# Two more buffers for the up weights, the last row tiles' sums ordered later, two norm factors later

## Chip, cores and metric

The kernel runs on one core of a Trainium2 chip. The metric is the device time of one execution in microseconds. Before the change it took 2193.57 us (median of 3 runs, 2191.82 to 2195.93).

## The reference

One inference step of a two-layer decoder of width 1024, for a prompt of 1024 tokens and 8 single decode tokens (1032 columns in all). Layer 0 mixes tokens by gated linear attention beside cross-attention into 256 memory tokens; layer 1 by sliding-window attention, again beside memory attention, with keys and values projected from the residual stream after layer 0. After each mixer stands a squared-ReLU MLP of width 4096 between two norms, and the change touches this MLP alone:

```python
def squared_relu_mlp(h, w_up, w_down):
    return jnp.square(jax.nn.relu(h @ w_up)) @ w_down
...
    f = squared_relu_mlp(rmsnorm(x, norm_ffn_pre[l]), w_ffn_up[l], w_ffn_down[l])
    x = x + rmsnorm(f, norm_ffn_post[l])
```

## The kernel before

Activations lie feature-major: 128 partitions by 8 feature tiles by token columns. Every float32 operand is split into a high part (a cast, `split` L157, on ScalarE) and a low part (source minus high part, on VectorE), and every product is three matmuls: high by high, high by low, low by high.

`mlp` (L678) is called once per layer. Its up product first makes 4 of the 32 row tiles of the hidden width directly (`up_plain`, L708) and stores the squared ReLUs in `apd`. The other 28 row tiles are taken in 14 pairs by a Strassen-Winograd scheme of seven products on half the features and half the columns (516, in two pieces of 258). `XF` holds the seven combinations of activations, made by `steps` (L766). `items` (L828) runs over pairs and products. For each pair `prepare` (L831) loads two raw weight tiles `ws` of 512 KB (`wstage`, L227, a pool of two buffers) and lets `wino_weights` (L657) make the seven weight combinations one after another, in place in the raw tiles, each split into a slot of three weight buffers. So the raw tiles are free only after the pair's last split. `prepare` runs up to five products ahead. `product` (L840) issues the 24 matmuls (L820 to L822) of one product into six rotating PSUM banks and the evictions (L641 to L655) on VectorE and ScalarE. After a pair, `factors` (L856) makes three more combinations of the pair's four result rows on VectorE, and `store` (L863) writes all seven into `awd` in DRAM. During pairs 2 to 4 `square_mean` (L727) also computes statistics of the residual.

The four direct row tiles need their combinations too. `plain_factors` (L871) is a generator: for each of two groups it loads four tiles `c` from `apd` (L875), makes four sums (L882) and stores each into `awd` (L883). It is advanced once per phase of the down product, in the first 13 phases.

The down product runs 64 phases (`phase`, L1034): six products of 8 phases over the hidden width with all 516 columns (48 matmuls per phase, L1050 to L1052), and one product in two column halves (`s` = 0 and 1, 8 phases of 24 matmuls each). Each phase needs a row tile `ra` read back from `awd` (`load_a`, L965, two buffers, asked for three phases ahead) and a weight tile `wr` (`load_w`, L978, five ahead; the first two lie in the same two-buffer pool as `ws`). `prep` (L986) splits both, two phases ahead. `gather` (L1016) adds the finished products into four accumulators.

The end of the MLP is the post-norm, done in four pieces pa to pd (`Closing`, L327), each of which squares its piece, sums over partitions by a matmul with ones (`Stats.mean`, L195, matmul L205), finishes the inverse root (`finish`, L210) and then scales and adds the residual (`close`). `hook` (L1085) starts these in given phases of the last product.

The order of the work is set by a list scheduler at compile time. It takes instructions by priority (program order, moved forward in `high_priority` blocks) on a model of the engines; each engine and each DMA queue then executes its list in order. Two means bend this order. A manual dependency marked NOSYNC adds no semaphore: it only keeps an instruction behind another one in the scheduler's order. `tick` (L127) uses it: `Stats.mean` is given a number of matmul columns, and its matmul is put behind the matmul in which that number has been counted down. One unit is 3 x 8 x 384 = 9216 columns. All the loads and stores named here are issued by SyncE's queue (SP).

Of the kernel before, what the change touches and what calls it, by code (L numbers as in the profile page):

```python
# [8 lines left out]
F32 = mybir.dt.float32  # L9
# [7 lines left out]
P = 128  # L17
# [19 lines left out]
PAIRS = [(m, m + 1) for m in range(NPL, DFF // P, 2)]  # L37
# [12 lines left out]
def hybrid_decoder_step(ctx: ExitStack, tc: tile.TileContext, A, O):  # L50
    nc = tc.nc
# [13 lines left out]
    rp = ctx.enter_context(tc.tile_pool(name="rstd", bufs=1))  # L65
# [26 lines left out]
    def nm(s):  # L92
        uid[0] += 1
        return f"{s}_{uid[0]}"
# [132 lines left out]
    def wstage(src, pool=None):  # L227
        with tc.high_priority(WPRI):
            ws = (pool or wp).tile([P, KT, P], F32, tag="ws", name=nm("ws"))
            nc.sync.dma_start(ws, src)  # L230
            return ws
# [446 lines left out]
    def mlp(l, X, ff):  # L678
# [4 lines left out]
        left, right = ff.left, ff.right  # L683

        def pool(st, side, name, bufs=1):
            return st.enter_context(tc.tile_pool(name=nm(name), bufs=bufs, side=side, reuse_waits="tile"))
# [21 lines left out]
        def up_plain(c):  # L708
            hl = X[c][0]
            c0, n = CH[c]  # L710
            for m in range(NPL):
                ps = mmps()
                proj(ps, W[m], hl, n, low_last=(m == NPL - 1))
                with first():
                    t = tmp3([P, 2, n])
                    nc.scalar.activation(t[:, 0, :], ps[:, :n], AF.Relu)
                    nc.scalar.activation(t[:, 1, :], t[:, 0, :], AF.Square)
                    if c < 2:
                        nc.sync.dma_start(apd[l, :, m, c, :384], t[:, 1, :])
                    else:  # L720
                        nc.sync.dma_start(apd[l, :, m, :, 384:], t[:, 1, :].rearrange("p (h w) -> p h w", h=2))
# [23 lines left out]
        def home(pool, tag, n=4):  # L745
            return pool.tile([P, n, HALF], F32R, tag=tag, name=nm("xf"))

        def cut(i, b, p):
            hi, lo = XF[i]
            eng = nc.vector  # L750
            p = pieces[p]
            for j in range(2):
                ks = slice(2 * j, 2 * j + 2)
                src = p[b][:, ks, :]
                if not isinstance(lo, list):
                    split(hi[:, ks, p["at"]], lo[:, ks, p["at"]], src, eng)
                    continue
                nc.scalar.copy(hi[:, ks, p["at"]], src)
                for k in (2 * j, 2 * j + 1):
                    eng.tensor_tensor(lo[k][:, p["at"]], p[b][:, k, :], f32(hi[:, k, p["at"]]), ALU.subtract)  # L760
# [5 lines left out]
        def steps(p):  # L766
            cut(1, "b11", p)
            comb(p, "b12", "b22", "b12", ALU.subtract)
            yield
            cut(7, "b12", p)  # L770
            comb(p, "b11", "b12", "b11", ALU.add)
            yield
            if p == 0:
                s0 = home(xp, "xh0", 5)
                XF[6] = (home(fa, "t2h"), s0[:, :4])
                XF["s0"] = s0
            cut(6, "b11", p)
            comb(p, "b12", "b22", "b11", ALU.subtract)
            yield
            if p == 0:  # L780
                s0 = XF.pop("s0")
                s1, s2 = home(xp, "xl0", 5), home(xp, "xh1", 5)
                s3 = home(xp, "xl1", 5)
                XF[5] = (s1[:, :4], s2[:, :4])
                XF[2] = (s3[:, :4], [x[:, 4] for x in (s0, s1, s2, s3)])
            cut(5, "b12", p)
            yield
            cut(2, "b21", p)
            comb(p, "b21", "b11", "b21", ALU.subtract)
            yield  # L790
            if p == 0:
                XF[3] = (home(xp, "xh2"), home(xp, "xl2"))
            cut(3, "b22", p)
            yield
            if p == 0:
                ff.rest.close()
                t4 = pool(right, "right", "t4")
                XF[4] = (home(t4, "h"), home(t4, "l"))
            cut(4, "b21", p)
            yield  # L800

        up_plain(0)
        scale(0)
        scale(1)
# [21 lines left out]
            return t[:, SUB * s : SUB * s + SUB]  # L826

        items = [(j, i) for j in range(len(PAIRS)) for i in ORDER]  # L828
        ws, gens, made = {}, {}, [0]

        def prepare(upto):  # L831
            while made[0] < min(upto, len(items)):
                j, i = items[made[0]]
                made[0] += 1
                if j not in gens:
                    w1, w2 = (wstage(A["w_up"][l, m]) for m in PAIRS[j])
                    gens[j] = wino_weights(w1[:, :4], w1[:, 4:], w2[:, :4], w2[:, 4:], slots)
                ws[j, i] = next(gens[j])

# [31 lines left out]
        def plain_factors():  # L871
            for q in range(2):
                rows = [tp.tile([P, 768], F32, tag=tag, name=nm("c"))[:, :HALF] for tag in ("t3", "t3", "tq", "tq")]
                for r, (m, h) in zip(rows, ((0, 0), (0, 1), (1, 0), (1, 1))):
                    nc.sync.dma_start(r, apd[l, :, 2 * q + m, h, :])  # L875
                yield
                yield
                c11, c12, c21, c22 = rows
                for f_, r, a, b, op in ((1, c12, c22, c12, ALU.subtract), (4, c11, c12, c11, ALU.add),
                                        (6, c21, c11, c21, ALU.subtract), (5, c22, c22, c11, ALU.subtract)):  # L880
                    yield
                    TT(r, a, b, op)  # L882
                    nc.sync.dma_start(awd[l, f_, NJ - 1, :, q, :], r)  # L883
# [201 lines left out]
        def hook(v):  # L1085
            if -8 <= v < -4:
                split(*lasting(v + 8), reg(3, v + 8))
            if v == -4:
                pa.feed(0, 1, 2, 3)
            if v == 0:  # L1090
                rooms((pa, "xh0"), (pc, "xl0"))
                pa.factor(rp.tile([P, 384], F32, tag="rf", name=nm("rf")), 0.3 * unit)
            if v == 1:
                pb.feed(0, 1, 2, 3)
                pb.factor(rx, 2 * unit)
            if v == 2:
                pa.close(behind=kept["mm"])
            if v == 4 and not l:
                hl[0] = xtiles(0)
                pa.cut(hl)  # L1100
            if v == 5:
                rooms((pb, "xl2"))
                pb.close(behind=kept["mm"])
            if v == 7:
                pc.feed(2, 3, 0, 1)
                pc.factor(rb, 2.5 * unit)
            if v == 9:
                pc.close((2, 3, 0, 1), behind=kept["mm"])
            if v == 11:
                rooms((pd, "xh2"))  # L1110
            if v == 10 and not l:
                rt[0] = rtile(0)
                pa.measure(0, rt[0], 2.3 * unit, Ring())
            if v == 11 and not l:
                hl[1] = xtiles(1)
                pc.cut(hl)
                hl[2] = xtiles(2)
                pb.cut(hl)
# [10 lines left out]
        for t in range(N):  # L1129
            for u in ([3, 4, 5] if t == 0 else [t + 5]):  # L1130
                if u < N:
                    load_w(u)
            if t + 3 < N:
                load_a(t + 3)
            if t + 2 < N:
                with urgent(2) if t + 2 >= 6 * NJ else ExitStack():
                    prep(t + 2)
            if t < 13:
                next(plain, None)
            phase(t)  # L1140
            if l == 0 and t in folds:
                fold(folds.pop(t), kept["mm"])
            hook(t - 6 * NJ)

        st2.close()
        if l:
            with urgent(2):
                pd.finale()
                pd.factor(rp.tile([P, 384], F32, tag="rf", name=nm("rf"))[:, : pd.n], 0)
            pd.close()  # L1150
        else:
            xs = pool(st, "right", "xs", 3)
            mq = pool(st, "right", "mq", 2)
            pd.feed(2, 3, 0, 1)
            pd.factor(rp.tile([P, 384], F32, tag="rf", name=nm("rf"))[:, : pd.n], 2 * unit)
            pd.close((2, 3, 0, 1), xs)
            pd.cut(hl, (2, 3, 0, 1))
            rt[1] = rtile(1)
            pc.measure(1, rt[1], 4 * unit, mq)
            pd.measure(1, rt[1], 5 * unit, mq)  # L1160
            rt[2] = rtile(2)
            pb.measure(2, rt[2], 9 * unit, mq)
            pd.measure(2, rt[2], 10 * unit, mq)
            res = [(hl[c], rt[c]) for c in range(3)]
# [1052 lines left out]
```

## Time and profile before

| | |
|---|---|
| median of 3 runs | 2193.57 us |
| profiled execution, own time | 2196.19 us |
| its span | 2194.4 us |
| TensorE busy | 97% |
| VectorE busy | 68% |
| ScalarE busy | 49% |
| mean granted TensorE clock | 0.994 |
| up products of the pairs, layer 0 / 1 | 536.9 to 826.3 us / 1566.2 to 1851.5 us |
| down products, layer 0 / 1 | 828.0 to 1157.1 us / 1852.2 to 2179.8 us |

The times of the two last rows are the first and last starts of the matmuls of lines L820 to L822 and L1050 to L1052. In the profile "PE" is TensorE, "DVE" VectorE, "ACT" ScalarE, "SPq" the queue of SyncE, "PEclk" the granted clock as a share of the full one. In timelines a bracket gives the idle time of the engine ahead of the instruction and what ended it. In a view by windows each engine has its busy time and, in brackets, its instructions; then come PEclk, the mean share of the 16 DMA engines and GB/s.

### The profile page before, as it was taken

The page shows a single profiled execution, that of the slowest core. Times are in us where ns is not written, and L with a number is a line of the kernel's source. Part 1 is how long each engine was busy: PE and PEld are TensorE (multiplying, and loading weights), DVE is VectorE, ACT ScalarE, POOL GpSimd, SP SyncE. Part 2 cuts the span into 40 slices and gives each one's busy share as a digit, 9 for nine tenths or more (in the row PEclk, how much of TensorE's full clock was granted, in tenths as well). Part 3 has the DMA queues.
Part 4 walks back from the last instruction along what each step waited for, and adds up shares of the span by engine and source line. Part 5 has one row for each costly group of instructions (what it writes and reads, how often), then busy time and mean ns, then how long its engine had stood idle before and what let it go on. Part 6 is the DMA issues. An engine that isn't in the chain of part 4 may idle for free.

```text
span 2194.4 us, 41861 instructions
## 1 busy us (share of the span) xinstructions
PE 2137.5 (97%) x16918; PEld 2040.5 (93%) x16918; DVE 1502.1 (68%) x2839; ACT 1083.3 (49%) x2191; POOL 112.4 (5%) x170
## 2 busy tenths in 40 slices
PE   8999999999999999999999999899999999999997
PEld 6879999999999999999999878699999999999997
DVE  7546648668877677756787455747888777855767
ACT  6354536457645444334554354646655445333453
POOL 0012000000000000034000000200000000000001
PEclk9999999999999999999999999999999999999999
DMA  4422026542664449467355101424275446725344
GB/s 168 143 68 75 24 65 176 157 140 98 189 216 130 153 157 328 143 225 237 117 156 164 53 21 32 164 71 149 97 241 183 141 160 219 268 97 167 100 132 145
DMA packets 142823, 316.40 MB, mean 144 GB/s; under 512 B 15833, under 2 KB 58897, under 8 KB 142273
## 3 DMA queue, kind: packets, MB, share of 16 engines
q1 hardware_dynamic: 125216, 270.43, 38.6%
q0 software_dynamic: 8368, 30.42, 4.2%
q10 hardware_dynamic: 9040, 12.82, 1.6%
q8 instruction: 134, 2.20, 0.4%
q14 instruction: 65, 0.53, 0.1%
HBM read 220.97 MB, written 93.74 MB: 143 GB/s over the span
## 4 chain that ended last, share of the span: by engine, by line
PE 70%; DVE 11%; DMA 11%; ACT 5%; issue 3%; SPq 0%; DVEq 0%; ACTq 0%
PE mm L259 16%; PE mx L259 8%; DMA ws<-in_w_up 5%; PE mx L1050 5%; PE mx L1051 5%; PE mx L1052 5%; DVE wl L159 3%; PE mm L1050 2%; PE mm L1051 2%; PE mm L1052 2%; PE mx L820 2%; PE mx L821 2%; PE mx L822 2%; DMA ra<-awd 1%; ACT wh L158 1%
## 5 line engine op out<-in xcount | busy, mean ns | idle before, releaser
L158 ACT CAST wh<-ws 128x512 fp32r<-128x512 f32 (+1 forms) x258 | 184.1, 721 | 304.8 <-DVE ws L666 119.7
L820 PE MATMUL mx<-xf,wh 128*128 128x258 f32 x1048 | 297.9, 284 | 3.7 <-DVE aw L649 3.5
L821 PE MATMUL mx<-xf,wh 128*128 128x258 f32 x1048 | 295.6, 282 | 0.0
L822 PE MATMUL mx<-xf,wl 128*128 128x258 f32 x1048 | 295.5, 282 | 0.0
L259 PE MATMUL mm<-xh,wh 128*128 128x384 f32 (+1 forms) x864 | 282.0, 326 | 1.6 <-DVE acc L1032 1.1
L259 PE MATMUL mm<-xh,wl 128*128 128x384 f32 (+1 forms) x864 | 278.5, 322 | 0.0
L259 PE MATMUL mm<-xl,wh 128*128 128x384 f32 (+1 forms) x864 | 278.1, 322 | 0.0
L159 DVE TENSOR_TENSOR wl<-ws,wh 128x512 fp32r<-128x512 f32 (+1 forms) x258 | 208.6, 816 | 100.6 <-ACT wh L158 100.3
L158 ACT CAST wh<-wr 128x1024 fp32r<-128x1024 f32 x102 | 106.9, 1048 | 283.7 <-PE sx L1051 271.1
L1050 PE MATMUL mx<-sa,wh 128*128 128x258 f32 x840 | 239.2, 285 | 5.2 <-ACT sa L158 1.8
L159 DVE TENSOR_TENSOR wl<-wr,wh 128x1024 fp32r<-128x1024 f32 x102 | 125.4, 1229 | 171.0 <-ACT wh L158 170.6
L1051 PE MATMUL mx<-sa,wh 128*128 128x258 f32 x840 | 236.9, 282 | 1.8 <-DVE sa L159 1.8
L1052 PE MATMUL mx<-sa,wl 128*128 128x258 f32 x840 | 236.7, 282 | 0.0
L820 PEld LDWEIGHTS mx<-xf,wh 128*128 128x128 f32 x1048 | 197.6, 189 | 5.6 <-DVE aw L649 5.1
L821 PEld LDWEIGHTS mx<-xf,wh 128*128 128x128 f32 x1048 | 198.0, 189 | 0.4
L822 PEld LDWEIGHTS mx<-xf,wl 128*128 128x128 f32 x1048 | 197.9, 189 | 0.0
L259 PEld LDWEIGHTS mm<-xh,wh 128*128 128x128 f32 x864 | 162.8, 188 | 10.9 <-issue 7.5
L259 PEld LDWEIGHTS mm<-xh,wl 128*128 128x128 f32 x864 | 162.4, 188 | 7.5 <-issue 5.5
L259 PEld LDWEIGHTS mm<-xl,wh 128*128 128x128 f32 x864 | 162.8, 188 | 6.8 <-issue 6.0
L1050 PEld LDWEIGHTS mx<-sa,wh 128*128 128x128 f32 x840 | 159.4, 190 | 7.1 <-DVE aw L655 2.5
L159 DVE TENSOR_TENSOR sa<-ra,sa 128x1032 fp32r<-128x1032 f32 (+1 forms) x128 | 144.2, 1126 | 27.1 <-ACT sa L158 26.6
L1051 PEld LDWEIGHTS mx<-sa,wh 128*128 128x128 f32 x840 | 159.2, 190 | 2.3 <-DVE sa L159 2.2
(569 smaller groups left out, 5792.7 us busy)
## 6 DMA issues: line engine op xcount, KB each, us to landing
ra<-awd SPq DMA_DIRECT2D x92, 516.0 KB, 3.7
ws<-in_w_up SPq DMA_DIRECT2D x64, 512.0 KB, 4.4
wr<-in_w_downb SPq DMA_DIRECT2D x64, 512.0 KB, 6.0
awd<-aw SPq DMA_DIRECT2D x26, 1032.0 KB, 7.7
awd<-am SPq DMA_DIRECT2D x28, 774.0 KB, 9.2
ws<-in_w_in_a SPq DMA_DIRECT2D x20, 512.0 KB, 3.9
ws<-in_w_out SPq DMA_DIRECT2D x16, 512.0 KB, 3.6
t<-xd SPq DMA_DIRECT2D x20, 384.0 KB, 3.6
```

What stands on the lines that cost most here:

```text
L158: nc.scalar.copy(hi, src)
L159: (eng or nc.vector).tensor_tensor(lo, src, f32(hi), ALU.subtract)
L259: mm = nc.tensor.matmul(ps[:M, :n], w_[:, k, :M], x_[:, k, :], start=(i == 0), stop=(i == 3 * KT - 1))
L820: nc.tensor.matmul(ps, wh(k), xh, start=(k == 0), stop=False)
L821: nc.tensor.matmul(ps, wh(k), xl, start=False, stop=False)
L822: mm = nc.tensor.matmul(ps, wl(k), xh, start=False, stop=(k == n - 1))
L1050: nc.tensor.matmul(ps, wh[:, q, ms], h, start=(jj == 0 and q == 0), stop=False)
L1051: nc.tensor.matmul(ps, wh[:, q, ms], lo, start=False, stop=False)
L1052: mm = nc.tensor.matmul(ps, wl[:, q, ms], h, start=False, stop=end)
```

## The change

The up weights of pairs 1, 3, 5 and so on go into a second pool of two buffers, `wq`, which is opened where the last combination of activations gets its room. `fetch` loads a pair's two tiles, and once that pool is open, the preparation of pair j also asks for the tiles of pair j+1. Next, the loads in `plain_factors` are put, by NOSYNC dependencies, behind the last matmul issued so far, and the generator is advanced after the phase's matmuls where it was advanced before them. Last, the matmul of piece pc's norm factor is put behind 2.8 units of later columns where it was 2.5, and that of piece pd in layer 0 behind 2.7 where it was 2.

```diff
                 t4 = pool(right, "right", "t4")
                 XF[4] = (home(t4, "h"), home(t4, "l"))
+                stage[0] = pool(right, "right", "wq", 2)
             cut(4, "b21", p)
             yield
 
+        stage = [None]
         up_plain(0)
...
-        ws, gens, made = {}, {}, [0]
+        ws, gens, made, raw = {}, {}, [0], {}
+
+        def fetch(j):
+            if j not in raw and j < len(PAIRS):
+                raw[j] = [wstage(A["w_up"][l, m], stage[0] if j % 2 else None) for m in PAIRS[j]]
 
         def prepare(upto):
...
                 if j not in gens:
-                    w1, w2 = (wstage(A["w_up"][l, m]) for m in PAIRS[j])
+                    fetch(j)
+                    w1, w2 = raw[j]
+                    if stage[0]:
+                        fetch(j + 1)
                     gens[j] = wino_weights(w1[:, :4], w1[:, 4:], w2[:, :4], w2[:, 4:], slots)
...
                 for r, (m, h) in zip(rows, ((0, 0), (0, 1), (1, 0), (1, 1))):
-                    nc.sync.dma_start(r, apd[l, :, 2 * q + m, h, :])
+                    d = nc.sync.dma_start(r, apd[l, :, 2 * q + m, h, :])
+                    tc.add_manual_dep(d.ins, kept["mm"], NOSYNC, reason="behind later matmuls")
...
                 pc.feed(2, 3, 0, 1)
-                pc.factor(rb, 2.5 * unit)
+                pc.factor(rb, 2.8 * unit)
...
+            phase(t)
             if t < 13:
                 next(plain, None)
-            phase(t)
...
-            pd.factor(rp.tile([P, 384], F32, tag="rf", name=nm("rf"))[:, : pd.n], 2 * unit)
+            pd.factor(rp.tile([P, 384], F32, tag="rf", name=nm("rf"))[:, : pd.n], 2.7 * unit)
```

## The prediction

> **What bounds the kernel now.** The first two lines of the page come first: the span and the engines' busy shares.
>
> ```profile
> span 2194.4 us, 41861 instructions
> PE 2137.5 (97%) x16918; PEld 2040.5 (93%) x16918; DVE 1502.1 (68%) x2839; ACT 1083.3 (49%) x2191; POOL 112.4 (5%) x170
> ```
>
> TensorE (PE) is the bound, and the change removes no matmul, so only time that PE loses can be won. Busy time hides half of that loss, because a matmul that starts late is drawn longer. So I count matmuls by stage. The second view is busy time by windows, PE alone; "x" is the count. The windows are the middle and end of the up products and the first 13 us of the down products, of layer 0 and then of layer 1.
>
> ```profile
> 560.00:600.00 40.00, 40.00 (x336) 1.00 0.74 225
> 600.00:665.00 65.00, 62.32 (x503) 1.00 0.63 203
> 665.00:826.40 161.40, 160.19 (x1332) 1.00 0.47 152
> 826.40:840.00 13.60, 10.02 (x55) 0.75 0.89 347
> 1580.00:1645.00 65.00, 65.00 (x542) 1.00 0.67 216
> 1645.00:1851.60 206.60, 205.60 (x1705) 1.00 0.50 163
> 1851.60:1865.00 13.40, 9.61 (x60) 0.87 0.96 362
> ```
>
> The first row is a stretch without loss: 336 matmuls in 40 us, 8.4 per us, 0.119 us each. At that pace the other rows lack 43, 24, 59, 4, 30 and 53 matmuls, which is 5.1, 2.8, 7.0, 0.5, 3.6 and 6.3 us. Part of the up rows is no loss: three pairs of statistics matmuls per layer, one of them here from the chain of waits, take 0.65 us a pair where their count of two stands for 0.24.
>
> ```profile
> 622.58 0.65 PE sx L205 x2
> ```
>
> That takes off 3 x 0.4 = 1.2 us per layer. What is left is 6.7 us of loss in layer 0's up stage and 2.9 in layer 1's (9.6 together), and 7.0 + 6.3 = 13.3 us at the two changes from up to down. That is all this change can reach, apart from the norm factors below.
>
> Why PE loses in the up stage: the timelines of VectorE (DVE) and PE.
>
> ```profile
> 614.70 0.69 DVE L666 TENSOR_TENSOR ws<-ws,ws 128x512 f32<-128x512 f32 x1 [2.25 <-DMA ws<-in_w_up]
> 615.65 0.42 DVE L649 TENSOR_TENSOR aw<-mx,aw 128x258 f32<-128x258 f32 x1
> 616.12 0.39 PE L820 MATMUL mx<-xf,wh 128*128 128x258 f32 x1 [0.79 <-DVE aw L649]
> 637.58 0.69 DVE L666 TENSOR_TENSOR ws<-ws,ws 128x512 f32<-128x512 f32 x1 [3.62 <-DMA ws<-in_w_up]
> 639.00 0.39 PE L820 MATMUL mx<-xf,wh 128*128 128x258 f32 x1 [1.42 <-DVE aw L649]
> ```
>
> DVE works in order. The first combination of a pair's weights (L666) waits 2.25 and 3.62 us for the second up tile; the evictions (L649) stand behind it, PSUM banks stay full, PE waits 0.79 and 1.42 us. The chain of waits shows why this returns with each pair:
>
> ```profile
> 691.80 7.29 DMA ws<-in_w_up
> 712.06 7.30 DMA ws<-in_w_up
> ```
>
> One buffer's loop (load 7.3 us, then 13 us until the last split frees it) takes 20.3 us, while PE needs 14 x 12 = 168 matmuls x 0.119 = 20.0 us for a pair. The load decides by 0.3 us, and any disturbance is never made good.
>
> **The change part by part.**
>
> **Two more weight buffers.** Nothing is added on a computing engine: the same 28 weight loads of 512 KB per layer, half of them into new buffers, and each pair's issued when the pair before starts its preparation, which is when its own load would have been issued for that earlier pair. The 7.3 us load then has 20 us of cover, and L666 no longer waits; the loop left is PE's own. Bounds: from the page, the plain idle time ahead of the largest group of these matmuls, 3.5 us, and the whole count, 9.6.
>
> ```profile
> L820 PE MATMUL mx<-xf,wh 128*128 128x258 f32 x1048 | 297.9, 284 | 3.7 <-DVE aw L649 3.5
> ```
>
> Layer 0's worst stretch has L666 waits in front of it, so I stand nearer the count, but keep something for evictions behind splits: **-7 us**. With its cover gone, that is if the new buffers came free only when they are needed, the load would cost what it costs now, 9.6 us. At the start two pairs are fetched together (4 x 512 KB); if DVE waited once for this, the price is one wait as above, 2.25 to 3.62 us behind which PE loses 0.8 to 1.4.
>
> **What follows at the change from up to down.** The last pair (13) is odd, so it lies in the new buffers; the old two, where the first two down weights (wr) also go, come free a pair earlier. SyncE's queue (SP), ScalarE (ACT) and PE at that place, and the windows of DMA and of the clock:
>
> ```profile
> 812.99 0.33 SPq L982 DMA_DIRECT2D wr<-in_w_downb  x1
> 813.42 0.39 SPq L865 DMA_DIRECT2D awd<-aw  x1
> 814.81 0.33 SPq L982 DMA_DIRECT2D wr<-in_w_downb  x1
> 815.19 1.46 SPq L869 DMA_DIRECT2D awd<-am  x1
> 816.75 1.59 SPq L976 DMA_DIRECT2D ra<-awd  x2
> 826.87 1.05 ACT L158 CAST sa<-ra 128x1032 fp32r<-128x1032 f32 x1 [4.69 <-DMA ra<-awd]
> 827.97 0.39 PE L1050 MATMUL mx<-sa,wh 128*128 128x258 f32 x1 [1.37 <-ACT sa L158]
> 829.24 0.38 PE L1051 MATMUL mx<-sa,wh 128*128 128x258 f32 x1 [0.88 <-DVE sa L159]
> 816.00:826.00 10.00, 10.00 (x86) 10.00 (x85) 4.01 (x10) 2.33 (x3) 0.00 (x0) 1.00 1.05 347
> 828.00:836.00 8.00, 5.79 (x21) 4.65 (x22) 8.00 (x11) 7.31 (x10) 0.00 (x0) 0.60 0.81 315
> ```
>
> The first down product waits for its row tile ra. Its 10 us are queueing: 2 x 512 KB of wr, 1032 KB and 774 KB of stores and 2 x 516 KB of ra, 3.86 MB, share full DMA engines (share 1.05) at 347 GB/s: 11.1 us. With both wr gone a pair earlier, where the share is 0.47, 2.84 MB are left, 8.2 us: ra lands 2.9 us sooner, at 824. Cast (1.05) and low part (1.22, the row of such a split stands below) end at 826.2, and PE finishes its up products at 826.6 (827.97 less its wait of 1.37). The waits of 1.37 and 0.88 go. The later ones, for evictions queued behind those splits on DVE, shrink, and with them the stretch at clock 0.60, whose cost is the other half of the 7.0 us. Bounds per layer: nothing (the engines stay saturated with the stores) to all 7.0 and 6.3. I leave 2.4 us per layer, one split of 1.2 us between evictions at half clock: **-8.5 us** for both.
>
> [...]
>
> **Last row tiles' sums later.** Per layer 8 loads, 8 subtractions or additions and 8 stores (258 KB each) leave the up stage and go behind the first (four) and the seventh (four) down phase.
>
> ```profile
> L882 DVE TENSOR_TENSOR c<-c,c x16: 683/689/697, 619.1 to 1677.5; 128x516 f32<-128x516 f32 x16
> SPq L883 <- DVE aw L651: 9.6, 1, 9.6
> SPq L883 <- DVE c L882: 5.7, 3, 3.0
> 862.42 1.05 ACT L158 CAST wh<-wr 128x1024 fp32r<-128x1024 f32 x1 [3.69 <-PE sx L1051]
> 865.62 1.22 DVE L159 TENSOR_TENSOR sa<-ra,sa 128x1032 fp32r<-128x1032 f32 x1
> 866.00:872.00 6.00, 5.90 (x6) 1.00 0.93 350
> ```
>
> On DVE that is 8 x 0.69 = 5.5 us per layer out of the stage where it holds PE up, which is inside the 7 us above. In the down stage a phase is 48 matmuls, 5.7 us; its splits are ready 4.4 us after the weight slot frees (862.42 to 866.84) and are needed two phases after (11.4 us), so 7 us of slack hide 5.5 us even in the stretch where DVE is full (5.90 of 6 us). The 4.1 MB are 11.8 us of DMA at 350 GB/s, spread over 13 phases (74 us); the first quarter comes while the engines are near full (0.81 at 828 to 836, 0.93 at 866 to 872), but the row loads run three phases ahead. Cost **0**; bounds 0 and, without that cover, 5.5 us per layer on DVE, or the SP price in the last rival.
>
> **Norm factors later.** 0.3 units (unit: 9216 columns) is 4 groups of three matmuls, 1.4 us; 0.7 units is 6452 columns or 17 matmuls of 384 columns at 0.173 us, 2.9 us.
>
> ```profile
> 1143.75 0.70 PE L205 MATMUL sf<-rb,ones 128*128 128x258 f32 x2 [0.69 <-DVE rb L199]
> 1158.40 0.41 PE L259 MATMUL mm<-xh,wh 128*128 128x384 f32 x1 [1.06 <-DVE acc L1032]
> 1175.11 0.70 PE L205 MATMUL sx<-rf,ones 128*128 128x258 f32 x2 [2.27 <-DVE rf L199]
> 1186.09 2.46 DVE L159 TENSOR_TENSOR xl<-acc,xh 128x264 fp32r<-128x264 f32 x7 [0.74 <-ACT xh L158]
> 1187.51 0.34 PE L259 MATMUL sT<-xh,wh 128*128 128x384 f32 x1
> ```
>
> Both waits are in layer 0 and end: 0.69 < 1.4 and 2.27 < 2.9. But what hangs on these factors is late next. The factor of 1175.11 would start 0.6 us later by the clock (2.9 - 2.27); the last splits of the next stage's input (1186 to 1188.5) follow it through a full DVE, and PE takes up that second chunk at 1187.51, just as its splits arrive. PE gets there 2.3 us sooner and waits for it. Likewise the factor of 1143.75 moves 0.7 us later, and the end of its chain, an eviction behind it on DVE, already holds PE 1.06 us at 1158.40. Bounds: -3 us (both waits gone, other matmuls fill in) to +1.3 us (both chains late). I take the middle of the mechanism, **0**. In layer 1 no such wait shows, and 1.4 us of delay stays ahead of the last evictions.
>
> **The sum.** -7 - 8.5 + 0 + 0 = -15.5 us. The profiled execution took 2196.19 us (1.8 around the span): 2180.7. It lies 2.6 us above the median of the runs, 2193.57, so against the median the forecast is 2178; I say **2179 us**.
>
> **The rivals.** First, **the queue at the change of stages stays** (for: the stores still fill the engines there, and the order on SP may keep wr where it is; against: a buffer freed 20 us earlier). Then only the up stage gains: 2193.6 - 7 = 2186.6. Second, **all lost time comes back**: 9.6 + 13.3 + 3 = 26 us, 2168; for it speaks that PE runs whole stretches of 40 us without loss, against it that evictions still share DVE with splits. Third, **the loads come no sooner in effect**, since SP is in order and a load for the new buffers stands behind stores that wait for DVE: the L666 waits return elsewhere, 2191 to 2194. Fourth, on the other side, **SP is blocked in the down stage**: each of the 8 stores per layer waits in SP's queue for its DVE operation, with row and weight loads behind it. Before, four such waits took 15.3 us, 3.8 each. Eight in a row are 30 us per layer; above the 7 us of slack plus one phase (5.7) PE loses what remains, 18 us per layer, 36 in all, less 15.5: 2214. It decides only if the waits follow each other without the queue recovering; over 13 phases with 9 us between stores that is unlikely.
>
> **How the numbers follow.** The forecast has 0.50 (its own range 2174 to 2184), the first rival 0.20, the second 0.12, the third 0.11, the fourth and lesser stalls 0.07. The range 2168 to 2191 holds the forecast and the first two rivals with the bounds of the unknown costs, and the better edge of the third. Faster by over 0.2% (4.4 us, about what a measurement of this kernel can tell from no change): 0.50 + 0.20 + 0.12 = 0.82; within 0.2%: 0.11; slower: 0.07.
>
> **What would show it.** Right: no DVE L666 wait on ws of more than a few tenths; 600 to 665 us with 540 matmuls; wr issued some 20 us before the last aw store; ra landing in 7 us or less; no clock below 0.9 at the change of stages; the two L205 waits gone and a wait at the second chunk's first matmul instead. Wrong: wr still between the two stores; PE waiting for sa in the first 13 down phases; SP held for several us at L883 there; or the up rows as short of matmuls as now.

## The result

The changed kernel takes **2173.97 us** (median of 4 runs, 2170.10 to 2175.46) against 2194.75 us before (4 runs beside it, 2191.82 to 2201.47). The ratio is 0.9898, 95% interval 0.9872 to 0.9925: 1.0% faster. Its profiled execution took 2174.24 us, of which 2172.3 us are the span. The forecast was 2179.0 us with a range of 2168 to 2191, so the time lies inside, 5 us on the fast side and at the lower edge of the narrower range, 2174 to 2184, that went with the forecast's own chance.

The first lines of the page of the changed kernel, as before: the span and the busy shares.

```profile
span 2172.3 us, 41879 instructions
PE 2126.8 (98%) x16918; PEld 2034.8 (94%) x16918; DVE 1520.1 (70%) x2839; ACT 1090.2 (50%) x2191; POOL 112.2 (5%) x170
```

PE has the same 16918 matmuls and is drawn as busy for 10.7 us less, while the span fell by 22.1: the busy time shows only half of it. Where that happened is seen in the windows of PE alone, in the same stretches of layer 0 and layer 1 as before, shifted by what was gained up to there (columns: length, PE's busy time and matmuls, granted clock, DMA share, GB/s).

```profile
600.00:665.00 65.00, 65.00 (x541) 1.00 0.51 158
817.90:831.50 13.60, 13.60 (x117) 1.00 1.00 349
1632.70:1836.30 203.60, 203.60 (x1697) 1.00 0.46 153
1836.30:1849.70 13.40, 13.40 (x115) 1.00 1.01 353
```

At 8.4 matmuls per us the first 13.6 us of the down product should hold 114 matmuls. They held 55 and now hold 117, at clock 1.00 instead of 0.75; layer 1 has 115 of 113 where it had 60. The stretch from 600 to 665 us holds 541 of 546 (503 before), and the missing five are no more than the statistics matmuls take. No loss is left in these rows; the one of layer 1's up stage lacks 13 of 1710 matmuls, 1.6 us, of which the two statistics pairs in it make 0.8; the rest is within the rounding of the pace (one matmul more or less in the 40 us from which it was taken is 5 in this row). The whole span, cut at the first and last matmuls of the stages:

| stretch | before, us | after, us | difference |
|---|---|---|---|
| start to first up product of layer 0 | 536.9 | 534.5 | -2.4 |
| up products, layer 0 | 289.4 | 283.3 | -6.1 |
| change and down products, to the next stage's first matmul | 332.1 | 326.0 | -6.1 |
| next stage to first up product of layer 1 | 407.8 | 409.1 | +1.3 |
| up products, layer 1 | 285.3 | 283.3 | -2.0 |
| change, down products and end | 342.9 | 336.1 | -6.8 |

The sum is -22.1 us. No edit lies in the first row, and in the fourth only the norm's last factor. What differs in both is the granted clock: it was 0.50 for 3.4 us from 99.1 us on in the profile before and never in this row in the one after; in the fourth row it was 0.50 for 6.8 us before (from 1392.8 on) and for 10.2 us after (from 1377.9 on). Half the clock for 3.4 us is 1.7 us by estimate, most of the -2.4 and as much as the +1.3. Two executions of one kernel, the one with the sums alone below, lie 4.1 and 4.4 us apart in these two rows. So the edits' own gain is in the other four rows, 21.0 us.

The timeline of the changed kernel, with the rows that answer those of the stalls before: VectorE's first combination of a pair's weights, then SP's queue at the end of layer 0's up products and ScalarE's cast of the first row tile.

```profile
623.51 0.69 DVE L666 TENSOR_TENSOR ws<-ws,ws 128x512 f32<-128x512 f32 x1
...
779.54 0.33 SPq L992 DMA_DIRECT2D wr<-in_w_downb  x1
782.00 0.33 SPq L992 DMA_DIRECT2D wr<-in_w_downb  x1
...
799.79 0.37 SPq L874 DMA_DIRECT2D awd<-aw  x1
801.33 2.52 SPq L986 DMA_DIRECT2D ra<-awd  x2
...
808.73 1.05 ACT L158 CAST sa<-ra 128x1032 fp32r<-128x1032 f32 x1 [1.18 <-DMA ra<-awd]
```

L666 has no bracket: the tile is there. The two wr leave 20 and 18 us before the last aw store (before, 0.4 us ahead of it and 1.4 us behind it). The row tile is asked for at 801.33 and its cast starts at 808.73, 7.4 us later (before 10.1). The up products end at 817.9, the first down matmul's start. The cast therefore starts 9.2 us before PE needs its first down product; before, it started 0.3 us too late (826.87 against 826.6).

The norm's place, PE's timeline, where the prediction quoted waits of 0.69, 1.06 and 2.27 us:

```profile
1128.98 0.70 PE L205 MATMUL sf<-rb,ones 128*128 128x258 f32 x2 [0.33 <-DVE rb L199]
1143.84 0.41 PE L259 MATMUL mm<-xh,wh 128*128 128x384 f32 x1 [2.70 <-DVE acc L1042]
1158.71 0.70 PE L205 MATMUL sx<-rf,ones 128*128 128x258 f32 x2 [1.77 <-DVE rf L199]
1172.50 0.35 PE L259 MATMUL sT<-xh,wh 128*128 128x384 f32 x1
1181.89 0.39 PE L259 MATMUL sA<-xh,wh 128*128 128x264 f32 x1 [0.65 <-DVE kf L1846]
```

The two factor waits are shorter, not gone, the eviction's wait has grown from 1.06 to 2.70, and the second chunk (1172.50) waits for nothing.

### The profile page after: what moved, and what is told of

Its sections match the earlier page's. It is cut to its first block, busy times and chain, and to the rows that moved or that the text cites. A ratio compares the mean times of both kernels' runs of the same rounds, so it can differ in the third digit from the quotient of the medians.

```text
span 2172.3 us, 41879 instructions
## 1 busy us (share of the span) xinstructions
PE 2126.8 (98%) x16918; PEld 2034.8 (94%) x16918; DVE 1520.1 (70%) x2839; ACT 1090.2 (50%) x2191; POOL 112.2 (5%) x170
## 4 chain that ended last, share of the span: by engine, by line
PE 88%; DVE 4%; ACT 3%; DMA 3%; issue 1%; SPq 0%; DVEq 0%; ACTq 0%
PE mm L259 16%; PE mx L259 8%; PE mx L822 6%; PE mx L824 6%; PE mx L823 6%; PE mx L1060 5%; PE mx L1061 5%; PE mx L1062 5%; PE mm L822 3%; PE mm L824 3%; PE mm L823 3%; PE mm L1060 2%; PE mm L1061 2%; PE mm L1062 2%; PE sx L1060 1%
## 5 line engine op out<-in xcount | busy, mean ns | idle before, releaser
L1062 PEld LDWEIGHTS mx<-sa,wl 128*128 128x128 f32 x840 | 158.3, 188 | 0.0
```

Of the source, the lines that this page charges most:

```text
L1062: mm = nc.tensor.matmul(ps, wl[:, q, ms], h, start=False, stop=end)
```

## The experiments

All kernels do the whole computation. Losses at the change of stages are counted as in the prediction: matmuls missing in the first 13.6 us (layer 0) or 13.4 us (layer 1) after the end of the up products, by 8.4 per us.

**The three parts, one at a time.** The buffers alone (the kernel before with `wq` and `fetch`):

```diff
+                stage[0] = pool(right, "right", "wq", 2)
...
+                raw[j] = [wstage(A["w_up"][l, m], stage[0] if j % 2 else None) for m in PAIRS[j]]
...
+                    fetch(j)
+                    w1, w2 = raw[j]
+                    if stage[0]:
+                        fetch(j + 1)
```

> The kernel before with the two more weight buffers and the earlier loads alone. Theory (the wait for the second up tile on VectorE makes both the losses in the up stage and those at the change to the down product): nearly the whole gain, 18 to 21 us faster than before, the up stages without waits for evictions, the row tile landed before the up products end. Rival (the last row tiles' sums on VectorE and in SyncE's queue start the losses): less than 12 us faster, with waits left between 600 and 665 us.

Measured: 2175.57 us, ratio 0.9915 (0.9902 to 0.9928). That is 18.7 us of the 22.4 that the whole change brings by its ratio. Windows of PE:

```profile
600.00:665.00 65.00, 65.00 (x538) 1.00 0.65 211
1632.00:1837.00 205.00, 203.16 (x1688) 1.00 0.50 166
```

Layer 0's up stage is whole with the sums still in it (538 against 541), and both changes of stage are whole too. In layer 1 the 205 us lack 34 matmuls, 4.0 us, where the changed kernel's row lacks 13, 1.6 us. So 2.4 us stay there. The length of the up products (first to last matmul, as in the table above) says the same: with the buffers alone layer 0 takes 283.4 us (289.4 before, 283.3 after) and layer 1 takes 285.9 (285.3 before, 283.3 after). The buffers cure layer 0 and bring nothing in layer 1, where no L666 waits any more in this kernel either.

The sums of the last row tiles alone:

```diff
+                    d = nc.sync.dma_start(r, apd[l, :, 2 * q + m, h, :])
+                    tc.add_manual_dep(d.ins, kept["mm"], NOSYNC, reason="behind later matmuls")
...
+            phase(t)
             if t < 13:
                 next(plain, None)
-            phase(t)
```

> The kernel before with the last row tiles' sums ordered behind the first down phase, nothing else. Theory: 2 to 4 us faster, since the sums lengthen VectorE's lag only where they lie (4.4 us are lost in layer 0 between 600 and 665 us, of which I give them half), and the change of stages loses 6 to 7 us in each layer as before. Rival (the sums start the losses): 8 us faster or more, and the later pairs without waits. A third way: the sums cost in the down product what they save, no difference.

Measured: 2188.85 us (12 runs), ratio 0.9969 (0.9960 to 0.9979). Its profiled execution, 2200.77 us, was the longest of its runs, so the same kernel was run once more:

> The last row tiles' sums alone once more, for a second profile: the first measured 6.8 us less than before, of which its profile shows 3.3 in the stages that the sums touch. If the sums alone bring 6 to 7 us, a second profile shows the up stages at 5 us of loss or less in all and a change of stages of 5 to 7 us per layer, with the rest outside these stages; if the first profile was typical, the ratio is nearer 0.9985.

Measured: 2190.58 us (12 runs), ratio 0.9980 (0.9969 to 0.9992). Windows of PE of this second execution, which took 2190.56:

```profile
600.00:665.00 65.00, 64.20 (x526) 1.00 0.42 135
823.10:836.70 13.60, 10.36 (x59) 0.75 0.92 350
1846.10:1859.50 13.40, 10.96 (x61) 0.75 0.91 329
```

By the two ratios this part is worth 4.4 and 6.8 us alone, more than the 2 to 4 expected and less than the rival's 8; the second ratio is nearer to the 0.9985 that was to follow if the first profile was typical. In this second profile the up products take 287.5 us in layer 0 (289.4 before) and 283.3 in layer 1 (285.3 before, and no more than in the changed kernel), while the changes of stage lose 6.6 and 6.1 us as before. VectorE's waits for weights are still there without the buffers: L666 waits 2.04 us at 612.38 (at about this place the kernel before had 2.25), and 1.4 to 3.3 us at each of the last ten pairs of layer 1, whose up stage is whole all the same. So moving the sums doesn't cure the wait, it makes less of it reach PE, and in layer 1 nothing: by one profile of each kernel the loss there goes with the sums and not with the wait. Whether that is VectorE's 5.5 us of work or the 4.1 MB in the queues, these runs don't separate.

The norm factors alone:

```diff
-                pc.factor(rb, 2.5 * unit)
+                pc.factor(rb, 2.8 * unit)
...
-            pd.factor(rp.tile([P, 384], F32, tag="rf", name=nm("rf"))[:, : pd.n], 2 * unit)
+            pd.factor(rp.tile([P, 384], F32, tag="rf", name=nm("rf"))[:, : pd.n], 2.7 * unit)
```

> The kernel before with the two norm factors put later, nothing else. Theory (the wait moves to what hangs on the factor): within 2 us of before; the waits ahead of the two factors' matmuls shrink, the wait for the last sums' eviction at the start of the next stage grows from 1.06 us by about as much. Rival: 3 us faster, both waits gone and nothing in their place.

Measured: 2195.49 us (12 runs), ratio 0.9996 (0.9984 to 1.0009): nothing. PE's timeline shows why:

```profile
1145.02 0.70 PE L205 MATMUL sf<-rb,ones 128*128 128x258 f32 x2 [0.21 <-DVE rb L199]
1160.80 0.41 PE L259 MATMUL mm<-xh,wh 128*128 128x384 f32 x1 [3.61 <-DVE acc L1032]
1175.75 0.70 PE L205 MATMUL sx<-rf,ones 128*128 128x258 f32 x2 [0.32 <-DVE rf L199]
```

The three waits were 0.69 + 1.06 + 2.27 = 4.02 us and are 0.21 + 3.61 + 0.32 = 4.14 us: the factors' waits shrink by 2.4 us and the wait for the evictions of the last sums grows by 2.6. Behind the wait of 3.61 us the clock was 0.50 for 3.4 us, which it was not in the kernel before.

**Both without the factors** (the changed kernel with 2.5 and 2 units):

> The changed kernel with the two norm factors where they were before. Theory: within 2 us of the changed kernel; waits of 0.5 to 2.5 us ahead of the two factors' matmuls in layer 0 as before the change, and a wait of about 1 us for the last sums' eviction where the changed kernel has 2.7. Rival (the later factors gain): 2 to 3 us slower than the changed kernel.

Measured: 2171.87 us, ratio 0.9898 (0.9884 to 0.9912), the changed kernel's own ratio. The same place on PE:

```profile
1128.17 0.70 PE L205 MATMUL sf<-rb,ones 128*128 128x258 f32 x2 [1.67 <-DVE rb L199]
1142.21 0.41 PE L259 MATMUL mm<-xh,wh 128*128 128x384 f32 x1 [0.44 <-DVE acc L1042]
1158.21 0.70 PE L205 MATMUL sx<-rf,ones 128*128 128x258 f32 x2 [1.56 <-DVE rf L199]
```

Waits of 3.67 us here, 4.80 in the changed kernel (0.33 + 2.70 + 1.77). The stage from its first matmul to that of sA with 264 columns (1180.49 here, 1181.89 there) takes 38.28 us here and 38.05 there. Whether the factors cost the 1.1 us that these waits differ by, these runs can't tell.

**What decides at the change of stages: the two wr in the queue, or VectorE's wait at the last pair.** What the two kernels show of VectorE there, first before the change (the wait at the last pair, then the low part of the first row tile), then after it:

```profile
801.92 0.69 DVE L666 TENSOR_TENSOR ws<-ws,ws 128x512 f32<-128x512 f32 x1 [2.40 <-DMA ws<-in_w_up]
827.95 1.23 DVE L159 TENSOR_TENSOR sa<-ra,sa 128x1032 fp32r<-128x1032 f32 x1 [6.45 <-ACT sa L158]
...
811.28 1.22 DVE L159 TENSOR_TENSOR sa<-ra,sa 128x1032 fp32r<-128x1032 f32 x1
```

Before, VectorE stood idle for 6.45 us in front of that low part, and the last evictions of the up products stand behind it in its order: the last one started at 834.12, 7.5 us after the up products' end. After, it started at 818.12, 0.2 us after their end. Three kernels take the two possible reasons apart. First, the changed kernel with the pairs' buffers swapped, so that the last pair lies in the old ones and wr must wait for it:

```diff
-                raw[j] = [wstage(A["w_up"][l, m], stage[0] if j % 2 else None) for m in PAIRS[j]]
+                raw[j] = [wstage(A["w_up"][l, m], None if j % 2 else stage[0]) for m in PAIRS[j]]
```

> The changed kernel with even pairs from the second on in the new buffers and odd pairs in the old ones: the last pair then lies where the first two down weights go, and these come as late as before, while its own load is still a pair ahead. Theory as predicted (the two down weights in front of the row tile in the full DMA queue): the row tile lands 3 us later than in the changed kernel, and a good part of the 6 to 7 us per layer at the change of stages returns: 8 to 12 us slower than the changed kernel. Rival (VectorE's lag at the last pair made stores and row tile late): the row tile still lands several us before the up products end, and the time is within 2 us of the changed kernel.

Measured: 2178.78 us, ratio 0.9929 (0.9916 to 0.9942). SP and ScalarE, then the windows:

```profile
801.67 0.34 SPq L992 DMA_DIRECT2D wr<-in_w_downb  x1
802.11 0.39 SPq L874 DMA_DIRECT2D awd<-aw  x1
804.14 0.35 SPq L992 DMA_DIRECT2D wr<-in_w_downb  x1
805.80 1.11 SPq L986 DMA_DIRECT2D ra<-awd  x2
815.42 1.06 ACT L158 CAST sa<-ra 128x1032 fp32r<-128x1032 f32 x1 [1.82 <-DMA ra<-awd]
```

```profile
819.80:833.40 13.60, 12.51 (x103) 1.00 1.01 357
1841.70:1855.10 13.40, 12.47 (x105) 1.00 1.01 362
```

The queue is again as it was before, wr around the store, and the row tile needs 9.6 us. The second wr waits for its buffer until 804.1, and the last store, whose tile VectorE had finished at 802.9, stands behind it in SP's queue and leaves at 804.53; the row tile's request follows that. Yet only 1.3 and 0.9 us are lost, not 7.0 and 6.3. The time fits neither expectation: it is 4.8 us above the changed kernel's by the medians and 6.8 by the ratios, where the prediction's reason asked for 8 to 12 us and VectorE's lag for at most 2. Of the 6.7 us between the two profiled spans, 2.4 lie at the two changes of stage and 4.3 ahead of the up products and between the layers, where executions of one kernel differ by as much.

Second, the opposite: the first two wr out of the queue, but the last pair's weights held back. In this kernel the second pool serves pair 13 alone, and its two loads wait for the last two low parts of pair 12; the other pairs use the old buffers, as before the change. The last-row sums and the factors stay as changed.

```diff
+                last = j == len(PAIRS) - 1
+                raw[j] = [wstage(A["w_up"][l, m], stage[0] if last else None, marks[x] if last else None)
+                          for x, m in zip((-2, -1), PAIRS[j])]
...
-                    if stage[0]:
-                        fetch(j + 1)
```

> The changed kernel without any load a pair sooner: all pairs in the old two buffers but the last, which lies in the new ones and whose two loads wait for the last splits of the pair before, as they did before the change. The down weights are early, VectorE's wait for the second up tile is back. Theory as predicted (the down weights' bytes): the two waits of 1.4 and 0.9 us for the row tile are gone, and the change of stages loses 2 to 3 us per layer where it lost 7.0 and 6.3. Rival (VectorE's lag): it loses 5 us or more per layer. In both the up stages lose 4 to 8 us in all; in time 10 to 13 us slower than the changed kernel by the first, 15 to 20 by the second.

Measured: 2185.80 us (6 runs), ratio 0.9953 (0.9940 to 0.9965). VectorE, SP, ScalarE and PE:

```profile
795.34 0.69 DVE L669 TENSOR_TENSOR ws<-ws,ws 128x512 f32<-128x512 f32 x1 [3.15 <-DMA ws<-in_w_up]
...
809.09 2.52 SPq L989 DMA_DIRECT2D ra<-awd  x2
818.05 1.05 ACT L159 CAST sa<-ra 128x1032 fp32r<-128x1032 f32 x1 [7.12 <-DMA ra<-awd]
819.13 1.23 DVE L160 TENSOR_TENSOR sa<-ra,sa 128x1032 fp32r<-128x1032 f32 x1 [4.40 <-ACT sa L159]
822.90 0.39 PE L1063 MATMUL mx<-sa,wh 128*128 128x258 f32 x1 [1.10 <-DVE aw L656]
```

```profile
821.20:834.80 13.60, 11.02 (x65) 0.75 0.89 323
1847.00:1860.40 13.40, 11.01 (x75) 0.87 0.91 333
```

With the first two wr gone 18 us and more before the store (at 787.06 and 788.82; the store left at 807.54), 5.9 and 4.5 us are lost. VectorE waited 3.15 us for the last pair's second tile, the store left late, ScalarE and VectorE stood idle for the row tile (7.12 and 4.40 us), and the last evictions of the up products came behind that. The cast started 3.2 us ahead of PE's end, so PE did not wait for the row tile itself: it waited for the evictions behind it, as the last row says. Against what was expected this is mixed: the loss in layer 0 is that of VectorE's lag (5 us or more), the one in layer 1 lies between, and the time, 11.8 us above the changed kernel's by the medians, is in the range given for wr (10 to 13). The profiled execution, 2189.80 us, was the longest of the six.

Third, the same kernel without the hold, so that pair 13 alone is fetched a pair ahead (the edit against the held kernel):

```diff
-                raw[j] = [wstage(A["w_up"][l, m], stage[0] if last else None, marks[x] if last else None)
+                raw[j] = [wstage(A["w_up"][l, m], stage[0] if last else None, None)
...
+                    if j == len(PAIRS) - 2:
+                        fetch(j + 1)
```

> As the kernel with the last pair held, but with the last pair's two loads a pair sooner; all other pairs in the old two buffers as before the change. If VectorE's lag at the last pair is what delays stores, row tile and evictions at the change of stages: the change of stages loses less than 1 us per layer where it lost 6.0 and 4.7 with the pair held, the up stages lose 3 to 6 us as there, and the time is 8 to 11 us under that of the held kernel. If the lag is carried in from earlier pairs: more than 3 us per layer stay.

Measured: 2177.69 us (6 runs), ratio 0.9924 (0.9906 to 0.9942). SP and ScalarE, then the windows:

```profile
808.12 2.54 SPq L991 DMA_DIRECT2D ra<-awd  x2
815.59 1.06 ACT L159 CAST sa<-ra 128x1032 fp32r<-128x1032 f32 x1 [1.68 <-DMA ra<-awd]
```

```profile
824.20:837.80 13.60, 13.60 (x116) 1.00 1.00 358
1842.30:1855.70 13.40, 13.40 (x115) 1.00 1.00 348
```

Both changes are whole: one pair loaded ahead, the last, takes away all that the held kernel loses there, and 8.1 us by the medians. The five kernels in one table (layer 0; the end of the up products is the start of each windows row, 826.6 before; the megabytes are the rate of a window from request to cast times its length):

| kernel | row tile asked for, ahead of that end | its cast starts, ahead of that end | time between | moved meanwhile | VectorE idle ahead of its low part | loss |
|---|---|---|---|---|---|---|
| before | 9.9 us | -0.3 us | 10.1 us | 3.57 MB | 6.45 us | 7.0 us |
| last pair held | 12.1 | 3.2 | 9.0 | 2.99 | 4.40 | 5.9 |
| last pair in old buffers | 14.0 | 4.4 | 9.6 | 3.35 | 1.70 | 1.3 |
| last pair ahead only | 16.1 | 8.6 | 7.5 | 2.52 | 0 | 0 |
| changed | 16.6 | 9.2 | 7.4 | 2.48 | 0 | 0 |

The loss follows VectorE's idle time, in layer 1 as well: 5.58, 3.07, 1.14, 0 and 0 us of it there go with losses of 6.3, 4.5, 0.9, 0 and 0. In the rows with clock 0.75 about half of the loss is the clock: a quarter of 13.6 us is 3.4. From before to after the cast gains 9.4 us on PE's end: 6.7 because the row tile is asked for earlier, 2.7 because it lands sooner. Of the 6.7 some 4 go with VectorE's wait at the last pair (9.9 to 14.0 with wr around the store, 12.1 to 16.1 by the hold alone) and 2.6 with the turn of wr in SP's queue (14.0 to 16.6). The time between request and cast follows the bytes that move meanwhile, at 334 to 353 GB/s; in the held kernel the next two wr leave SP at 814.54, during that transfer, and in the last two kernels of the table after it.

**The chain behind the last sums.** The factor of pd put later still:

```diff
-            pd.factor(rp.tile([P, 384], F32, tag="rf", name=nm("rf"))[:, : pd.n], 2.7 * unit)
+            pd.factor(rp.tile([P, 384], F32, tag="rf", name=nm("rf"))[:, : pd.n], 3.2 * unit)
```

> The changed kernel with the last piece's norm factor in layer 0 behind 3.2 units of columns where it has 2.7. Theory (what hangs on the factor is late next): its wait of 1.8 us goes, the next projection's second chunk of columns starts at most 0.5 us sooner, counted from the first matmul of the next stage, and a wait stands in front of it. Rival: the stage from the first to the second chunk is 1.5 to 2 us shorter. In time both are within 2 us of the changed kernel, so the trace decides.

Measured: 2178.33 us (6 runs), ratio 0.9922 (0.9910 to 0.9934), some 5 us worse than the changed kernel by the ratios. PE's timeline and one window:

```profile
1143.10 0.66 PE L259 MATMUL mm<-xh,wh 128*128 128x384 f32 x1 [2.49 <-DVE acc L1042]
1174.14 0.69 PE L259 MATMUL sT<-xh,wh 128*128 128x384 f32 x1 [2.69 <-ACT xh L158]
1186.54 0.39 PE L259 MATMUL sA<-xh,wh 128*128 128x264 f32 x1 [0.76 <-DVE kf L1846]
```

```profile
1174.00:1180.00 6.00, 5.86 (x18) 0.50 0.01 3
```

No wait on rf is left, and the second chunk's first matmul waits 2.69 us for its splits in its place. Expected was a time within 2 us of the changed kernel's. The stretch to sA grows from 38.05 to 43.44 us, 5.4 more. The wait on rf, 1.77 us, is gone; the new wait adds 2.69, and behind it 6 us hold 18 matmuls, where 0.173 us each would make 35, another 2.9. The remaining 1.6 us stand ahead of the factor's matmul: here the clock was also 0.50 for 3.1 us from the stage's first matmul on, behind its wait of 2.49 us, and in the changed kernel it stayed at 1.00 behind one of 2.70.

And the other end of it: the last four operations of the closing of pc (two multiplications, two additions) are ordered behind the second of the down product's last four evictions, which stand behind them on VectorE.

```diff
+                two = [TT(fk, fk, self.rf, ALU.mult), TT(fk, fk, xs, ALU.add)]
+                if i >= 2:
+                    self.rest += two
...
+        if not l:
+            for x in pc.rest:
+                tc.add_manual_dep(x.ins, kept["g", 1].ins.name, NOSYNC, reason="behind the last sums")
```

> The changed kernel with the second half of one piece's scaling and residual addition in layer 0 (four operations on VectorE) ordered behind the second of the last four evictions, which stand behind them now. If the wait of 2.7 us at the start of the next stage comes from that order: the wait falls under 0.7 us, and the time is 1 to 2.5 us less than the changed kernel's. Rival (the chain through the delayed operations becomes late): the wait moves to the second chunk of columns, and the time is the same.

Measured: 2173.66 us, ratio 0.9901 (0.9888 to 0.9914), the time of the changed kernel.

```profile
1142.71 0.41 PE L259 MATMUL mm<-xh,wh 128*128 128x384 f32 x1 [0.29 <-DVE acc L1044]
1153.27 0.55 PE L1865 MATMUL sf<-ident,t 128*128 128x128 f32 x3 [1.97 <-DVE t L1855]
```

The wait of 2.70 us falls to 0.29, a wait of 1.97 appears ten us later behind the moved additions, and the stretch to sA (at 1183.23) grows from 38.05 to 40.52 us: 2.4 us gained in front, 2.5 lost behind. Some 1.7 of the 2.5 are the clock, which was 0.50 for 3.4 us behind the new wait (from 1154.07 on) and 1.00 all through this place in the changed kernel. So the rows show a second wait in place of the first, and most of its price is a drop of the clock; that the delay as such must come back is not shown.

## Why the prediction was right, and where it was off

**Bound.** "Only time that PE loses can be won" held: 21.0 of the 22.1 us of span came from the stretches in which matmuls were missing, the other 1.1 from the two rows that differ by the clock.

**Two more buffers, -7.** Mechanism right in layer 0: L666 waits no more, 541 matmuls where 540 were asked for, and the buffers alone bring 6.0 of the 6.1 us. In layer 1 it is not what the runs show: the buffers alone bring nothing there, and the 2.0 us come with the sums. The gain of the up stage was 6.1 + 2.0 = 8.1 us, nearer to the count's end of the bounds, 9.6. What I kept back for evictions behind splits is not to be seen in the windows of the changed kernel. The double fetch at the start cost no wait of L666, and both layers' up products take the same 283.3 us.

**Last row tiles' sums.** "Cost 0 in the down stage" held: both first stretches of the down product are whole, and layer 1's down products take 321.7 us from the first to the last matmul with the sums among them and 321.6 without (the buffers alone). "Inside the 7" was true of the sum only: alone they bring 4.4 to 6.8 us, of which the second profile shows 1.8 + 2.1 in the two up stages. With the buffers they still add 2.4 us in layer 1's up stage by the profiles. By the two ratios (0.9915 and 0.9898) it is 3.7 us, but their intervals overlap.

**The change of stages, -8.5: the step that was mis-sized.** I kept "2.4 us per layer, one split of 1.2 us between evictions at half clock", because I let only the two wr leave the queue, with the row tile landing 2.9 us sooner after its request. That term measured 2.7 us. What I left out is that the same VectorE wait at the last pair also delays the store and the row tile's request, and that the evictions then stand behind an idle VectorE. The request comes 6.7 us earlier against PE's end, some 4 us of it by the end of that wait and 2.6 by wr leaving SP's queue ahead of the store. With wr back around the store most of the loss stays away (1.3 us), with wr out but the wait kept most of it returns (5.9 us). So wr in the queue, by its bytes and by its turn, is worth 0.9 to 1.3 us a layer by the windows once the loads are early, and the wait at the last pair the rest. Both losses, 13.3 us, came back: 4.8 us more than forecast, most of the 6.5 us between the sum, 2180.7, and the profiled 2174.24. That the total still came within 5 us owes something to luck: the largest term had its smaller cause priced and its larger one left out. Of the signs, wr and the clock came as stated; the row tile took 7.4 us where 7 or less were asked for.

**Norm factors, 0.** The size held (0.9996 alone). The place didn't: I named both spots where the waits could go, and expected the two L205 waits gone and one at the second chunk instead. Of these only the eviction at the next stage's first matmul took wait over (1.06 to 2.70); the second chunk waits only from 3.2 units on, and the two L205 waits stayed, 0.33 and 1.77. The kernel without the factors has 1.67 and 1.56 there, where before it was 0.69 and 2.27, so the other two parts shift them by about as much as the factors do.

**The rivals.** The second, all lost time back (2168), was the nearest in mechanism: up and change came back whole, and only its 3 us for the factors did not. It had 0.12, too little, given that the same L666 wait stood at the root of layer 0's loss in the up stage and of both changes. The first (the queue stays) and the third (loads no sooner) are ruled out by the wr rows and the L666 row. The fourth, SP blocked in the down stage, did not come. SP's waits at the stores of the sums, by groups (sum, count, longest):

```profile
SPq L893 <- DVE c L892: 10.2, 10, 2.8
```

They are 10.2 us over both layers, 5.1 in each, where the prediction's 15.3 before were those of layer 0 alone, and none is longer than 2.8, well under the 7 us of slack.

## What to carry to other kernels

A load that arrives late in each round (here VectorE waited 1.2 to 3.6 us for it) can cost little where it stands and much at the end of the stage, because the evictions behind it, the stage's last store and the next stage's first load inherit the delay (the buffers alone bring nothing in layer 1's up stage and make its change of stages, which had lost 6.3 us, whole); so follow a wait to the next stage before pricing its removal. Count matmuls per window at the undisturbed pace rather than busy time to see what such a loop costs and whether anything is left. And a wait removed by a later ordering constant is gained only when what hangs on the moved work isn't late next (with 3.2 units the wait of 1.77 us went and one of 2.69 us came).

## What the runs showed of the hardware that was not expected

The clock fell after waits of 2.49 and 2.69 us in the kernel with 3.2 units and after one of 1.97 us in the one with the last sums first; before the change it fell at 829.55 us, behind waits of 1.37 and 0.88 us close together. It did not fall in the changed kernel after one of 2.70 us. So the length of the single wait does not sort these cases.

PE's busy time around the first matmul of the next stage, in the kernel with 3.2 units and then in the changed one, in stretches as long as the one at clock 0.50, 3.41 us:

```profile
1139.36:1142.77 3.41, 1.25 (x11) 1.00 1.08 393
1142.77:1146.18 3.41, 3.08 (x10) 0.50 0.89 246
...
1139.01:1142.42 3.41, 2.12 (x18) 1.00 0.92 290
1142.42:1145.83 3.41, 1.99 (x11) 1.00 0.92 325
```

With 3.2 units the stretch that holds most of the wait of 2.49 us is idle for 2.16 us, and the clock is 0.50 in the next. The longer wait of 2.70 us, in the changed kernel, lies in two stretches, idle for 1.29 and 1.42 us, and the clock stays at 1.00. These idle times are estimates, taken from the ends of the matmuls as the profile draws them. So a wait of about the same length went with a stretch at half clock in one kernel and with none in the other; what decides it, these runs do not show.

The time between a row tile's request and its cast, 7.4 to 10.1 us in the five kernels, went with the bytes that moved meanwhile, 2.48 to 3.57 MB at 334 to 353 GB/s (the table above). The held kernel took 1.5 us longer than the one with the last pair ahead only and moved 0.47 MB more, which is 1.4 us at its 334 GB/s.
